# Tree-masked attention: normalising all slots in one operation and overwriting the exchanged halves

## The chip, the cores and the metric

The kernel runs on one core of a Trainium2 chip. The metric is device time in microseconds for one execution. A profile of one execution is at hand for the kernel before; its lines name the engines PE (TensorE matmul), PEld (TensorE weight load), DVE (VectorE), ACT (ScalarE), POOL (GpSimd) and SP (SyncE).

## The reference

The problem is attention with a fixed mask. There are 8 batches of 12 heads, 512 positions and 64 features per head. Positions are the nodes of a binary heap, and a position sees itself and its ancestors only.

```python
for i in range(seq):
    mask[i, i] = 1
    parent = i
    while parent > 0:
        parent = (parent - 1) // 2
        mask[i, parent] = 1
scores = np.einsum('bhqd,bhkd->bhqk', Q, K) * scale
scores = scores + (1 - mask) * (-1e9)
weights = np.exp(scores - np.max(scores, axis=-1, keepdims=True))
weights = weights / (np.sum(weights, axis=-1, keepdims=True) + 1e-10)
return np.einsum('bhqk,bhkd->bhqd', weights, V).astype(np.float32)
```

## The kernel before

Query `n = 4p + t` lies on partition `p` (0 to 127) in slot `t` (0 to 3). Two heads of one batch are worked on together. Such a couple is called a pair: 8 batches of 6 pairs make 48, numbered by `i`, and `hp` is the pair's number within its batch.

For each pair there are three functions:

- `transposes(i)` turns Q and K of the pair with 16 TensorE matmuls against permutation matrices (L274). VectorE copies the Q result to `qt` (L296), ScalarE the K result to `kt` (L297). At the first pair of a batch it also issues the batch's loads (`load`, L223) on POOL's queue: Q and K by parts of the heads, V one batch ahead, with a cast from fp32 to bf16.
- `scores(i)` makes masked scores for a shared set of 128 keys (`st1`) and for four further sets, one for each column block (`stx`). A matmul with code matrices writes a large negative number where the mask forbids (L310). ScalarE takes the exponentials into `et1` (L323) and `etx` (L334).
- `values(i)` multiplies the exponentials with V into one PSUM tile `o2` (32 matmuls, L352). V has a column of ones beside its 64 features, so each slot gets 65 columns, the last of them the sum of the weights. VectorE takes the reciprocals of the 8 sums of each partition (`rec`, L358). It multiplies each slot's 64 features by them into the fp32 tile `of` (L364). SP's queue writes `of` to the output (L369).

The queries' columns have one peculiarity. On partitions 0 to 63, columns 0 and 1 are exchanged:

```python
def _slot(c, p):

    return 1 - c if c < 2 and p < 64 else c
```

The normalisation at L361 to L368 puts them back in order, with one operation for columns 2 and 3 of all partitions, one for columns 0 and 1 of partitions 64 to 127, and one for columns 0 and 1 of partitions 0 to 63 in reversed order.

VectorE also spreads V into the tiles `v1` and `vx` for the next batch (`spread` and `copies`, L259): ten copies over six pairs.

The order on PE, VectorE, ScalarE and POOL is the program's own (`manual_schedule`). For each `i` it is `scores(i + 1)`, `transposes(i + 3)`, `values(i)`, then a share of the spread copies. The PSUM pools have one buffer for each tile, so the matmuls of `values(i + 1)` wait until the multiplies of `values(i)` have read `o2`. The pool of `rec` and `of` has four buffers, the pool of loaded Q, K and V six, and the spread V tiles are three.

Of the kernel before, what the change touches and what calls it, by code (L numbers as in the profile page):

```python
# [126 lines left out]
def kernel(  # L127
# [8 lines left out]
    B, H, S, D = Q.shape  # L136
    P = nc.NUM_PARTITIONS
# [203 lines left out]
    def values(i):  # L341
        b, hp = pairs[i]
        v1, vx = v1s[b % NV], vxs[b % NV]
        et1, etx = state.pop(i)
        o2 = psumO.tile([P, 2, 512], fp32)
        for hi in range(2):
            h = 2 * hp + hi
            for t in range(T):
                w = [(et1[:, hi, P * t:P * t + P], v1[:, h, 0:D + 1]),
                     (etx[:, hi, t, :], vx[:, h, t, 0:D + 1])]  # L350
                for n, (e, v) in enumerate(w):
                    nc.tensor.matmul(  # L352
                        out=o2[:, hi, (D + 1) * t:(D + 1) * (t + 1)],
                        lhsT=e, rhs=v, start=n == 0, stop=n == len(w) - 1,
                    )
        o4 = o2[:, :, 0:T * (D + 1)].rearrange("p h (t x) -> p h t x", t=T)
        rec = opool.tile([P, 2, T, 1], fp32)
        nc.vector.reciprocal(out=rec[:, :, :, :], in_=o4[:, :, :, D:D + 1])  # L358
        of = opool.tile([P, 2, T * D], fp32)
        of4 = of[:, :, :].rearrange("p h (t d) -> p h t d", t=T)  # L360
        for p0, p1, c0, t0 in ((0, P, slice(2, 4), slice(2, 4)),  # L361
                               (64, P, slice(0, 2), slice(0, 2)),
                               (0, 64, slice(1, None, -1), slice(0, 2))):
            nc.vector.tensor_tensor(  # L364
                out=of4[p0:p1, :, t0, :], in0=o4[p0:p1, :, c0, 0:D],
                in1=rec[p0:p1, :, c0, :].to_broadcast([p1 - p0, 2, 2, D]),
                op=ALU.mult,
            )  # L368
        nc.sync.dma_start(  # L369
            out=out[b, 2 * hp:2 * hp + 2].rearrange(  # L370
                "h (p t) d -> p h (t d)", t=T
            ),
            in_=of[:, :, :],
        )
# [3 lines left out]
    with tc.manual_schedule(engines={E.PE, E.DVE, E.Activation, E.Pool}):  # L378
        transposes(0)
        scores(0)  # L380
        transposes(1)
        copies(spread(0, 0, 6))
        transposes(2)
        for i in range(N):
            b, hp = pairs[i]
            if i + 1 < N:
                scores(i + 1)
            if i + 3 < N:
                transposes(i + 3)
            values(i)  # L390
            if b == 0:
                if hp in (0, 3):
                    todo = spread(0, 6, H) if hp == 0 else spread(1, 0, H)
                copies(todo[4 * (hp % 3):4 * (hp % 3) + 4])
            elif b + 1 < B:
                if hp == 0:
                    todo = spread(b + 1, 0, H)
                cuts = (0, 1, 2, 4, 6, 8, 10)
                copies(todo[cuts[hp]:cuts[hp + 1]])
# [30 lines left out]
```

## Time and profile before

| | |
|---|---|
| median of 5 executions | 162.08 us (162.0 to 163.41) |
| the profiled execution | 161.85 us, of which its span is 159.7 us |
| DVE busy | 128.5 us (80% of the span), 339 instructions |
| PE busy | 110.5 us (69%) |
| ACT busy | 107.9 us (68%) |
| POOL busy | 38.7 us (24%) |
| multiplies of L364 | 144, 60.9 us busy |
| bytes moved by the DMA engines | 32.28 MB |

The span runs from the first to the last instruction. The device time of the same execution is 2.15 us longer. A row of digits in the profile cuts the span into 40 equal slices and gives the busy share of each slice in tenths. A row of a group gives, behind its name, tiles and shape, the number of instructions, then the busy time in us and the mean in ns, then the idle time of the engine just before them and what ended it. A row of a timeline gives the start, the duration, the engine, the line and the tiles, and in brackets how long the engine had been idle and what released it. In a merged row (x3) the duration runs from the first start to the last end.

### The profile page before, as it was taken

To read this page: it belongs to the slowest core of one execution; us is meant where nothing else is said; L and a number is where in the kernel's file an instruction comes from. 1 tells how busy PE (TensorE), PEld (TensorE's weight loads), DVE (VectorE), ACT (ScalarE), POOL (GpSimd) and SP (SyncE) were. 2 spreads that over 40 slices of the span, in tenths; PEclk is the share of its full clock that TensorE was granted. 3 is DMA by queue.
4 is the path that set the end of the run, shared out by engine and by line. 5 is a ranking of instruction groups with operands and counts; after the bars stand their busy time and mean duration, and the time that the engine had idled before them with its cause. 6 is when DMAs were issued, how large, how long until landed. Compare 5 with 4: busy or idle time off the path is not lost.

```text
span 159.7 us, 5230 instructions
## 1 busy us (share of the span) xinstructions
PE 110.5 (69%) x2208; PEld 78.3 (49%) x2208; DVE 128.5 (80%) x339; ACT 107.9 (68%) x145; POOL 38.7 (24%) x49
## 2 busy tenths in 40 slices
PE   0427598658787769776885598776977788679630
PEld 0214375445555546554664376554655565546320
DVE  2108579899899989997999869998999899987751
ACT  3142467684598679956987568867996698759810
POOL 7955441422212322033222242223201000000000
PEclk9999999996999999999999969999999999999995
DMA  5999999999999999999999999999999999331331
GB/s 132 125 179 197 197 199 219 224 221 219 222 233 231 235 230 226 238 231 231 223 233 232 226 239 221 223 236 226 224 240 224 235 226 234 119 135 66 135 131 66
DMA packets 50951, 32.28 MB, mean 202 GB/s; under 512 B 1520, under 2 KB 50800, under 8 KB 50928
## 3 DMA queue, kind: packets, MB, share of 16 engines
q0 software_dynamic: 37584, 18.88, 87.7%
q1 hardware_dynamic: 13344, 13.08, 28.5%
q8 instruction: 17, 0.28, 0.6%
q14 instruction: 6, 0.05, 0.1%
HBM read 38.24 MB, written 12.58 MB: 318 GB/s over the span
## 4 chain that ended last, share of the span: by engine, by line
DMA 54%; DVE 30%; PE 7%; issue 5%; POOL 2%; DVEq 0%; POOLq 0%
DMA ks<-in_K_dram 54%; DVE of L364 18%; PE o L352 5%; DVE vx L259 4%; DVE rec L358 3%; DVE v L259 3%; DVE qt L296 2%; POOL qs L223 1%; PE st L310 1%; POOL vs L223 1%; PE tk L274 0%; POOL ks L223 0%; PE stx L310 0%; PE tq L274 0%; DVEq L425 0%
## 5 line engine op out<-in xcount | busy, mean ns | idle before, releaser
L323 ACT ACTIVATE et<-st 128x1024 bf16<-128x1024 f32 x48 | 49.2, 1024 | 29.5 <-PE st L310 28.7
L364 DVE TENSOR_TENSOR of<-o,rec 128x256 f32<-128x256 f32 x144 | 60.9, 423 | 3.0
L352 PE MATMUL o<-v,et 128*128 128x65 bf16 x384 | 30.9, 196 | 25.5 <-DVE of L364 19.6
L352 PEld LDWEIGHTS <-et 128*128 128x128 bf16 x384 | 25.1, 98 | 32.9 <-DVE of L364 23.6
L334 ACT ACTIVATE etx<-stx 128x768 bf16<-128x768 f32 x48 | 38.6, 804 | 0.0
L297 ACT COPY kt<-tk 128x512 bf16<-128x512 bf16 x48 | 28.4, 591 | 14.3 <-PE tk L274 14.3
L352 PE MATMUL o<-vx,etx 128*128 128x65 bf16 x384 | 30.6, 195 | 0.0
L296 DVE COPY qt<-tq 128x512 bf16<-128x512 bf16 x48 | 20.3, 423 | 12.4 <-PE tq L274 11.2
L274 PE MATMUL tq<-ptile,qs 128*64 128x128 bf16 x384 | 21.4, 237 | 12.3 <-DMA qs<-in_Q_dram 8.7
L259 DVE COPY vx<-vs 32x1536 bf16<-32x1536 bf16 (+3 forms) x54 | 28.3, 525 | 1.2
L352 PEld LDWEIGHTS <-etx 128*128 128x128 bf16 x384 | 25.8, 99 | 0.0
L274 PE MATMUL tk<-ptile,ks 128*64 128x128 bf16 x384 | 20.8, 231 | 6.3 <-DMA ks<-in_K_dram 6.0
L310 PEld LDWEIGHTS <-kt 64*128 64x128 bf16 x480 | 19.2, 99 | 10.8 <-issue 2.2
L223 POOL DMA_DIRECT2D qs<-in_Q_dram x18 | 15.1, 840 | 36.2 <-DMA vs<-in_V_dram 15.7
L274 PEld LDWEIGHTS <-qs 128*64 128x64 bf16 x384 | 14.9, 116 | 15.8 <-DMA qs<-in_Q_dram 9.6
L223 POOL DMA_DIRECT2D ks<-in_K_dram x18 | 14.8, 825 | 30.1 <-DMA ks<-in_K_dram 11.1
L310 PE MATMUL st<-ctile 64*128 64x512 bf16 x96 | 19.8, 409 | 0.0
L310 PE MATMUL st<-qt,kt 64*128 64x512 bf16 x96 | 19.5, 402 | 0.1
L274 PEld LDWEIGHTS <-ks 128*64 128x64 bf16 x384 | 14.9, 117 | 7.8 <-DMA ks<-in_K_dram 7.4
L358 DVE RECIPROCAL rec<-o 128x8 f32<-128x8 f32 x48 | 9.6, 200 | 9.8 <-PE o L352 9.8
L310 PE MATMUL stx<-qt,kt 64*128 64x96 bf16 x384 | 17.0, 211 | 0.0
L310 PE MATMUL stx<-ctile 64*128 64x384 bf16 x96 | 16.7, 343 | 0.0
(11 smaller groups left out, 33.5 us busy)
## 6 DMA issues: line engine op xcount, KB each, us to landing
out_dram<-of SPq DMA_DIRECT2D x48, 256.0 KB, 6.2
qs<-in_Q_dram POOLq DMA_DIRECT2D x14, 384.0 KB, 26.3
ks<-in_K_dram POOLq DMA_DIRECT2D x14, 384.0 KB, 26.5
vs<-in_V_dram POOLq DMA_DIRECT2D x7, 768.0 KB, 27.6
vs<-in_V_dram POOLq DMA_DIRECT2D x2, 384.0 KB, 9.0
qs<-in_Q_dram POOLq DMA_DIRECT2D x2, 256.0 KB, 17.1
ks<-in_K_dram POOLq DMA_DIRECT2D x2, 256.0 KB, 17.5
ctile<-tree_codes SPq DMA_DIRECT2D x1, 288.0 KB, 2.8
```

What stands on the lines that cost most here:

```text
L223: nc.gpsimd.dma_start(out=dst[:, h0:h1, :], in_=src[n, h0:h1].rearrange("h (p t) d -> p h (t d)", t=T),)
L259: nc.vector.tensor_copy(out=o, in_=i)
L274: nc.tensor.matmul(out=o[D * hi:D * hi + D], rhs=perms[mat], lhsT=src[:, 2 * hp + hi, D * t:D * t + D], start=True, stop=True, is_transpos ...
L296: nc.vector.tensor_copy(out=qt[:, :], in_=tq[:, :])
L297: nc.scalar.copy(out=kt[:, :].rearrange("d (i j x) -> d i j x", j=2, x=32), in_=tk[:, :].rearrange("d (j i x) -> d i j x", j=2, x=32)[:, 0:8],
L310: nc.tensor.matmul(out=dst, lhsT=lhsT, rhs=rhs, start=first, stop=True, skip_group_check=not first,)
L323: nc.scalar.activation(out=et1[:, :, :], in_=st1[:, :, :], func=AF.Exp, scale=scale)
L334: nc.scalar.activation(out=etx[:, :, :, 32:P], in_=stx[:, :, 0:384].rearrange("p h (c q) -> p h c q", c=T), func=AF.Exp, scale=scale,)
L352: nc.tensor.matmul(out=o2[:, hi, (D + 1) * t:(D + 1) * (t + 1)], lhsT=e, rhs=v, start=n == 0, stop=n == len(w) - 1,)
L358: nc.vector.reciprocal(out=rec[:, :, :, :], in_=o4[:, :, :, D:D + 1])
L364: nc.vector.tensor_tensor(out=of4[p0:p1, :, t0, :], in0=o4[p0:p1, :, c0, 0:D], in1=rec[p0:p1, :, c0, :].to_broadcast([p1 - p0, 2, 2, D]), ...
```

## The change

Two of the three multiplies are merged. One operation now normalises all four slots of all 128 partitions, in the columns' own order. On partitions 0 to 63 this leaves columns 0 and 1 in each other's slots. A second operation then writes these two slots of partitions 0 to 63 again, in reversed order, over what the first wrote.

```diff
-        for p0, p1, c0, t0 in ((0, P, slice(2, 4), slice(2, 4)),
-                               (64, P, slice(0, 2), slice(0, 2)),
+        for p0, p1, c0, t0 in ((0, P, slice(0, 4), slice(0, 4)),
                                (0, 64, slice(1, None, -1), slice(0, 2))):
             nc.vector.tensor_tensor(
                 out=of4[p0:p1, :, t0, :], in0=o4[p0:p1, :, c0, 0:D],
-                in1=rec[p0:p1, :, c0, :].to_broadcast([p1 - p0, 2, 2, D]),
+                in1=rec[p0:p1, :, c0, :].to_broadcast([p1 - p0, 2, t0.stop, D]),
                 op=ALU.mult,
             )
```

## The prediction

> **What bounds the kernel now.** I read the page first: the span, the busy shares and the two rows of slices (each slice is 159.7 / 40 = 4.0 us).
>
> ```profile
> span 159.7 us, 5230 instructions
> ...
> PE 110.5 (69%) x2208; PEld 78.3 (49%) x2208; DVE 128.5 (80%) x339; ACT 107.9 (68%) x145; POOL 38.7 (24%) x49
> ...
> DVE  2108579899899989997999869998999899987751
> ...
> DMA  5999999999999999999999999999999999331331
> ```
>
> Two things are nearly full at once: the transfers until slice 34 (136 us), and VectorE over most of the same stretch. Only where VectorE is what ends last does a shorter normalisation count. So I asked for the groups with shapes kept apart, to price an operation, and for VectorE's timeline, to see how operations follow one another.
>
> ```profile
> L364 DVE TENSOR_TENSOR of<-o,rec 64x256 f32<-64x256 f32 x96 | 40.5, 422 | 1.3
> ...
> L364 DVE TENSOR_TENSOR of<-o,rec 128x256 f32<-128x256 f32 x48 | 20.4, 424 | 1.6
> ```
>
> Half the partitions cost the same: 422 against 424 ns. What counts is elements per partition, 256 in each of the three.
>
> ```profile
> 68.69 0.42 DVE L296 COPY qt<-tq 128x512 bf16<-128x512 bf16 x1
> 69.03 0.20 DVE L358 RECIPROCAL rec<-o 128x8 f32<-128x8 f32 x1
> 69.26 1.30 DVE L364 TENSOR_TENSOR of<-o,rec 128x256 f32<-128x256 f32 x3
> 70.48 0.70 DVE L259 COPY v<-vs 32x768 bf16<-32x768 bf16 x2
> ...
> 145.56 0.21 DVE L358 RECIPROCAL rec<-o 128x8 f32<-128x8 f32 x1 [0.42 <-PE o L352]
> 145.81 1.30 DVE L364 TENSOR_TENSOR of<-o,rec 128x256 f32<-128x256 f32 x3
> ```
>
> Three multiplies take 1.30 us, so 3 x 0.424 and about 13 ns between them. The reciprocal starts 0.34 us after a copy of 0.42 us: it depends on nothing in it and overlaps it by 0.08 us. The multiply that reads `rec` starts 0.03 us after the reciprocal has ended.
>
> Then TensorE, for what holds it, late in the run:
>
> ```profile
> 125.41 0.41 PE L274 MATMUL tk<-ptile,ks 128*64 128x128 bf16 x8 [0.75 <-DMA ks<-in_K_dram]
> 126.06 0.20 PE L352 MATMUL o<-v,et 128*128 128x65 bf16 x1 [0.24 <-DVE v L259]
> ...
> 144.87 0.20 PE L352 MATMUL o<-v,et 128*128 128x65 bf16 x1 [0.19 <-DVE of L364]
> ...
> 149.45 0.20 PE L352 MATMUL o<-v,et 128*128 128x65 bf16 x1 [0.76 <-DVE of L364]
> ```
>
> At 125.4 us it waits for a K load (batch 6, heads 6 to 11: issued at 97.22, 28.1 us to landing, so 125.3). The same wait stands at 74.07 (1.58 us) and 91.23 (1.72 us). From there to the end its waits are for VectorE. The chain of waits gives one period of the end, 145.54 to 147.83: PE `o` 0.67, `rec` 0.22, the multiplies 1.30, joints 0.10, together 2.29 us with nothing beside it, since `o` has one buffer.
>
> So: up to pair 36 (batch 6, `hp` 0) the loads set the pace at the middle of each batch, VectorE in between. POOL issues a new load about 0.5 us after an older one lands, with some 25 us of loads queued, so a faster VectorE cannot pull loads forward. From pair 36 on VectorE sets the end.
>
> **The change part by part.** Per pair, removed: three multiplies of 256 elements per partition. Added: A, all partitions, 512 elements; C, partitions 0 to 63, 256 elements, on top of what A wrote. Elements per partition stay at 768; one instruction's fixed part goes. C is the old third multiply, 0.424.
>
> A has no row. By the trace, its floor is the line through the reciprocal (8 elements, 198 ns) and the multiply: 0.91 ns an element, so 657 ns; its ceiling is twice 424, 848 ns. [...]
>
> The joint between A and C is the unknown. C overwrites A, so an order between them may be enforced by a wait on VectorE's own count. Nearest row: reciprocal to multiply, +0.03 us after the end. If no wait is made, both start at partition 0 and the nearest row is copy to reciprocal, -0.08. I take +0.03: 0.691 + 0.030 + 0.424 = 1.145 us against 1.299, **0.154 us saved per pair**. With -0.08 it would be 1.035, 0.264 saved. Queued behind C on VectorE are the spread copies, the next `qt` and the next reciprocal; waiting for C are `values` of the next pair on PE and the output DMA on SP. All move earlier by the saving.
>
> [...]
>
> In all VectorE is relieved of 48 x 0.154 = 7.4 us. What reaches the end:
> - Pairs 0 to 35: nothing. The loads cover it: the K loads for pairs 18, 24 and 36 already arrive after TensorE asked for them, and the one for pair 30 lands at 108.1 where its scores' turn comes at about 109. If that cover were gone, 36 x 0.154 = 5.5 us more.
> - Pair 36: its K transposes end at 125.41 + 0.41 = 125.82, then 0.24 us of waiting for VectorE's copies, which are now earlier: up to 0.24 gained. Against that, outputs are written earlier and share the DMA engines: at most some 0.6 of a pair's output ahead, and one output takes 0.7 us of all engines (slices of 3 tenths over a 2.3 us period), so 0 to 0.4 us of delay. Net 0.
> - Pairs 36 to 47: 12 x 0.154 = 1.85 us. The next load (K of batch 7, issued 106.18, landing 132.5) allows pair 39's reciprocal from about 133.6; it would come at 134.67 - 3 x 0.154 = 134.2. The last two K loads land at 136.8 and 138.8, needed at 141 and later.
> - Limits in pairs 42 to 44: TensorE has 0.19 us to spare per pair, enough for 0.154 but not 0.264. ScalarE's three operations run back to back there (`et` starts at 143.88, 146.16, 148.46: 2.29 us), so it falls behind by 0.15 a pair; the score buffers are free 0.56 us ahead (`et` read by 144.90, written again at 145.46), enough for three such pairs. After pair 44 there is no `kt` and it has slack again.
>
> Sum: 0 + 1.85, about 1.9 us. The profiled execution took 161.85 us (span 159.7 and 2.15 around it), so 159.95; the median shown is 162.08, 0.23 above it: **160.2 us**.
>
> SP's output issues keep their number and size, POOL has no instruction moved, and `rec` and the DMA wait on the `of` buffer stay ahead of the first multiply.
>
> **The rivals.**
> (a) No wait is made between A and C. 12 x 0.264 = 3.2, less 0.1 each in pairs 42 to 44: 2.9 us, 159.2. For it: that overlap is in the trace between independent operations. Against: A and C write the same bytes, and the one dependent pair that the trace has waits.
> (b) The end is held elsewhere: ScalarE's 2.29 us holds pairs 42 to 44 (0.46 lost) or loads land 0.4 to 0.5 us later. 1.4 us, 160.7. [...]
> [...]
> That the change removes an instruction is plain from the code; it cannot fail to.
>
> **How the numbers follow.** A measurement here tells 0.5%, 0.8 us, from no change. Forecast 0.52; (a) 0.22; (b) at 160.7 0.12; (b) with all its losses 0.09; (c) 0.05. Faster by over 0.5% (below 161.27): 0.52 + 0.22 + 0.12 = 0.86; same 0.09; slower 0.05. The range runs from a little below (a), 158.7, to where (b) has most of its losses, 161.4; only (c) and the ends are left out.
>
> **What would show it.** [...] VectorE busy down by about 48 x 0.157 = 7.5 us to 121. K loads of batches 4 to 6 landing within 0.5 us of 91.2, 108.1 and 125.3, with longer TensorE waits in front of them. Period in the last pairs 2.14 instead of 2.29. I would be wrong if loads landed earlier (a gain near 5 us) or if the joint were above 0.1 us.

## The result

The changed kernel takes 160.9 us (median of 44 executions) against 162.31 us (median of 79). The ratio is 0.9933, 95% interval 0.9916 to 0.995, so about 1.1 us faster. Some executions of every kernel lie over 1.5% above its fastest; the ratios, and the table of profiles below, leave them out. Two later measurements gave 0.9905 (0.9867 to 0.9943) and 0.9893 (0.9848 to 0.9937), 1.5 and 1.7 us. The forecast was 160.2 us, 1.9 us faster. The direction and the range held; the forecast gain was 0.2 to 0.8 us larger than those measured.

From the page of the kernel after: the lines that answer to those shown of before, the group of the K transposes, and the row of TensorE's granted clock (in tenths of full speed, one digit for each 4 us):

```profile
span 159.3 us, 5182 instructions
...
PE 114.3 (72%) x2208; PEld 82.4 (52%) x2208; DVE 121.9 (76%) x291; ACT 107.4 (67%) x145; POOL 37.9 (24%) x49
...
DVE  2109289899699989996799799985899489988651
...
PEclk9999999999599999998799999996999779999975
DMA  5999999999999999999999999999999999332331
...
L274 PE MATMUL tk<-ptile,ks 128*64 128x128 bf16 x384 | 21.4, 236 | 10.4 <-DMA ks<-in_K_dram 10.1
```

The same clock row and the same group in the page of the kernel before:

```profile
PEclk9999999996999999999999969999999999999995
...
L274 PE MATMUL tk<-ptile,ks 128*64 128x128 bf16 x384 | 20.8, 231 | 6.3 <-DMA ks<-in_K_dram 6.0
```

VectorE is relieved: its busy time falls from 128.5 to 121.9 us. The loads end in the same slice, and TensorE waits for K for 10.1 us in all instead of 6.0. What was not expected is in the clock row: more slices in which TensorE ran below full speed. PE is busy for longer (114.3 against 110.5 us) with the same 2208 matmuls.

The two groups of multiplies of the kernel after, by shape:

```profile
L363 DVE TENSOR_TENSOR of<-o,rec 128x512 f32<-128x512 f32 x48 | 33.2, 692 | 1.7
...
L363 DVE TENSOR_TENSOR of<-o,rec 64x256 f32<-64x256 f32 x48 | 20.0, 416 | 1.6
```

The large multiply takes 692 ns where 691 was expected. VectorE's timeline of the kernel after, in the last pairs:

```profile
145.55 0.21 DVE L358 RECIPROCAL rec<-o 128x8 f32<-128x8 f32 x1 [0.42 <-PE o L352]
145.79 1.14 DVE L363 TENSOR_TENSOR of<-o,rec 128x512 f32<-128x512 f32 x2
...
147.69 0.21 DVE L358 RECIPROCAL rec<-o 128x8 f32<-128x8 f32 x1 [0.42 <-PE o L352]
```

The two multiplies take 1.14 us together, in place of 1.30, and one pair follows the other after 2.14 us, in place of 2.29. So the operation and the chain at the end are priced rightly. Yet the profiled span is only 0.4 us shorter.

One term has to be put straight first. A step `i` is the turn of the program's loop that ends in `values(i)`; the transposes in it are those of pair `i + 3`. So what the prediction calls the K load for pair 36 is the load that TensorE waits for in step 36, ahead of `values(36)`; pair 39 is the first to use it. The sums do not depend on the name.

Here is what happened on TensorE, from its timeline after, and below it the last pair's line from the timeline before:

```profile
125.60 0.54 PE L274 MATMUL tk<-ptile,ks 128*64 128x128 bf16 x8 [2.14 <-DMA ks<-in_K_dram]
...
153.49 0.21 PE L352 MATMUL o<-v,et 128*128 128x65 bf16 x1 [1.57 <-DVE of L363]
```

```profile
154.12 0.19 PE L352 MATMUL o<-v,et 128*128 128x65 bf16 x1 [1.72 <-DVE of L364]
```

The K load of step 36 lands about when it did before (125.5 us; 125.3 before), but TensorE now waits 2.14 us for it instead of 0.75. (The loads of steps 24 and 30 land at 90.4 and 107.6 us, against 91.2 and 108.1.) The view by windows shows what follows the waits. A line gives the window, its length, the busy time and instructions of PE, PEld, VectorE, ScalarE and POOL, then the granted clock, the DMA share and GB/s:

```profile
90.40:94.40 4.00, 3.91 (x86) 2.88 (x86) 2.98 (x8) 2.89 (x5) 1.55 (x2) 1.00 1.32 237
107.60:111.60 4.00, 3.99 (x65) 2.90 (x66) 2.30 (x5) 2.60 (x4) 1.07 (x2) 0.64 1.33 238
125.60:129.60 4.00, 4.00 (x59) 2.79 (x60) 2.13 (x5) 1.98 (x3) 0.00 (x0) 0.57 1.30 243
129.60:133.60 4.00, 3.96 (x92) 2.96 (x89) 3.45 (x9) 3.65 (x6) 0.00 (x0) 1.00 1.30 231
153.40:154.60 1.20, 1.04 (x16) 0.90 (x16) 0.03 (x1) 0.00 (x0) 0.00 (x0) 0.50 0.27 96
```

Behind waits of 2.47 us (at 107.6) and 2.14 us (at 125.6) the clock is 0.64 and 0.57 over 4 us; behind one of 1.46 us (at 90.4) it is 1.00. In the last pair it is 0.50: its value matmuls take 1.05 us instead of 0.66. There the wait is not longer than before (1.57 against 1.72 us), so length alone cannot be the cause. The kernel before had one such stretch late in the run, at 91.2.

### The profile page after: what moved, and what is told of

It is laid out like the page before. It is cut to its first block, busy times and chain, and to the rows that moved or that the text cites. A ratio compares the mean times of both kernels' runs of the same rounds, so it can differ in the third digit from the quotient of the medians.

```text
span 159.3 us, 5182 instructions
## 1 busy us (share of the span) xinstructions
PE 114.3 (72%) x2208; PEld 82.4 (52%) x2208; DVE 121.9 (76%) x291; ACT 107.4 (67%) x145; POOL 37.9 (24%) x49
## 4 chain that ended last, share of the span: by engine, by line
DMA 74%; DVE 10%; PE 7%; POOL 3%; issue 3%; POOLq 0%
DMA qs<-in_Q_dram 40%; DMA ks<-in_K_dram 34%; DVE of L363 6%; PE o L352 4%; PE st L310 1%; DVE vx L259 1%; DVE rec L358 1%; POOL vs L223 1%; POOL qs L223 1%; POOL ks L223 1%; DVE v L259 1%; PE stx L310 1%; PE tk L274 1%; PE tq L274 1%; DVE qt L296 1%
## 5 line engine op out<-in xcount | busy, mean ns | idle before, releaser
L363 DVE TENSOR_TENSOR of<-o,rec 128x512 f32<-128x512 f32 x96 | 53.2, 554 | 3.3
L352 PE MATMUL o<-v,et 128*128 128x65 bf16 x384 | 32.7, 201 | 18.1 <-DVE of L363 11.8
L352 PEld LDWEIGHTS <-et 128*128 128x128 bf16 x384 | 26.7, 102 | 25.4 <-DVE of L363 16.2
L352 PE MATMUL o<-vx,etx 128*128 128x65 bf16 x384 | 32.4, 200 | 0.0
L274 PE MATMUL tq<-ptile,qs 128*64 128x128 bf16 x384 | 21.9, 240 | 11.6 <-DMA qs<-in_Q_dram 7.4
L274 PE MATMUL tk<-ptile,ks 128*64 128x128 bf16 x384 | 21.4, 236 | 10.4 <-DMA ks<-in_K_dram 10.1
L352 PEld LDWEIGHTS <-etx 128*128 128x128 bf16 x384 | 27.6, 102 | 0.0
L223 POOL DMA_DIRECT2D qs<-in_Q_dram x18 | 14.6, 813 | 35.5 <-DMA qs<-in_Q_dram 9.6
L274 PEld LDWEIGHTS <-ks 128*64 128x64 bf16 x384 | 15.4, 120 | 11.9 <-DMA ks<-in_K_dram 11.5
```

Source lines behind the costliest of these rows:

```text
L223: nc.gpsimd.dma_start(out=dst[:, h0:h1, :], in_=src[n, h0:h1].rearrange("h (p t) d -> p h (t d)", t=T),)
L274: nc.tensor.matmul(out=o[D * hi:D * hi + D], rhs=perms[mat], lhsT=src[:, 2 * hp + hi, D * t:D * t + D], start=True, stop=True, is_transpos ...
L352: nc.tensor.matmul(out=o2[:, hi, (D + 1) * t:(D + 1) * (t + 1)], lhsT=e, rhs=v, start=n == 0, stop=n == len(w) - 1,)
L363: nc.vector.tensor_tensor(out=of4[p0:p1, :, t0, :], in0=o4[p0:p1, :, c0, 0:D], in1=rec[p0:p1, :, c0, :].to_broadcast([p1 - p0, 2, t0.stop, ...
```

## The experiments

Three theories of the missing part were tried. Theory 1: the clock falls behind the longer waits for K. Theory 2: the loads land later, since outputs are written earlier. Theory 3: it is mainly the last pair's slow matmuls. ("Rival 3" in e2 and e3 is another idea: that the pairs before 36 carry the gain.)

**e1, the change again.**

> The changed kernel again, beside which the others of this group are read. Theory 1 (clock): the longer waits for K loads let TensorE's granted clock fall to about half for some 4 us afterwards, and this takes back part of the 1.85 us; the time is 0.6 to 0.8% below before. In the profile the waits of TensorE for K at pairs 18, 24, 30 and 36 are 1.5 to 2.5 us, and the windows of 4 us behind those over about 1.9 us have a clock near 0.6. Theory 2 (loads): the clock plays no part; the K loads of batches 5 to 7 land 0.5 us or more later than in the kernel before and every window has a clock of 1.

Measured: ratio 0.9905. Its profile has clocks of 0.53 and 0.50 behind waits for K of 2.42 and 2.32 us, and 1.00 behind one of 0.92. K lands at 90.7, 108.3 and 124.8 us (91.2, 108.1 and 125.3 before): no delay by 0.5 us. One execution of each would be thin evidence, since the load of step 36 lands anywhere between 124.6 and 127.4 us in the fourteen profiles. But its mean is 125.7 us in the four kernels whose first 36 pairs are the old ones and 125.8 in the other ten, so nothing supports theory 2. Over the executions of this group the mean clock was 0.947 with the change and 0.966 before.

**e2, the change in pairs 36 to 47 only, and e3, in pairs 0 to 35 only** (`i < 36` in the same line; `old` holds the three multiplies, `new` the two).

```diff
-        for p0, p1, c0, t0 in ((0, P, slice(0, 4), slice(0, 4)),
-                               (0, 64, slice(1, None, -1), slice(0, 2))):
+        for p0, p1, c0, t0 in (new if i >= 36 else old):
```

> The change for pairs 36 to 47 only; pairs 0 to 35 have the three old multiplies. Theory 1 (clock): up to pair 36 the waits for K stay as short as before, so the clock falls no more often than before, and the 12 pairs bring 1.85 us less at most 0.4 for a slow last pair: 1.4 to 1.9 us faster than before, 0.3 to 0.8 us faster than the full change. Theory 2 (loads): outputs of the first 36 pairs are no longer early, so loads land as before: the full 1.85 us as well, but the clock is the same in both kernels. Rival 3 (the early pairs carry the gain): under 0.4 us faster than before.

> The change for pairs 0 to 35 only; pairs 36 to 47 have the three old multiplies. Theory 1 (clock): no gain from the pairs themselves, and slower stretches behind longer waits for K: 0.3 us faster to 1 us slower than before, with a clock near 0.6 in two or more of the windows behind the K waits of pairs 18, 24, 30 and 36. Theory 2 (loads): 0 to 0.5 us slower with the clock at 1. Rival 3 (the early pairs carry the gain): 1 us or more faster than before.

Measured: e2 0.9949 (0.9916 to 0.9982), e3 1.0032 (0.9996 to 1.0067). The 36 early pairs alone bring nothing, as the forecast had it for them; whether they lose is within the interval. The mean clock of e3 is 0.951, and its profile has clocks of 0.72 and 0.57 behind waits for K of 2.66 and 1.95 us. Rival 3 falls. But e2 is 0.8 us faster, not 1.4 to 1.9, and not faster than the full change. In its profile the stretch is as expected, with the clock whole in both places that the full change had lost:

```profile
125.90:128.40 2.50, 2.46 (x55) 1.78 (x56) 1.40 (x5) 1.45 (x2) 0.00 (x0) 1.00 1.32 235
152.62:154.00 1.38, 0.64 (x16) 0.52 (x16) 0.67 (x2) 0.00 (x0) 0.00 (x0) 1.00 0.45 161
```

That execution had a mean clock of 0.98; the mean over e2's executions is 0.966, and those with a higher clock were the faster ones (correlation with the span -0.70). The profile shows a better case than the median. The mean clock does not settle it, though: 0.966 is that of the kernel before as well, and over the 39 executions of the change that the first ratio counts the correlation is only -0.29.

**e4, fillers for TensorE in all these places; e5, at the K waits only; e6 and e10, ahead of the last pair only.** (In the first part of the diff `i` is the pair that is transposed: steps 18, 24, 30 and 36.)

```diff
+        if i in (21, 27, 33, 39):
+            for n in range(20):
+                put(tk[:, 0:128], qs, n % T, 0)
         for t in range(T):
             at = kput[t][1]
...
+        if i == N - 1:
+            tq = psumT.tile([P, 512], bf16)
+            for n in range(16):
+                for hi in range(2):
+                    nc.tensor.matmul(
+                        out=tq[D * hi:D * hi + D, 0:128], rhs=perms[0],
+                        lhsT=loaded[b][0][:, 2 * hp + hi, 0:D],
+                        start=True, stop=True, is_transpose=True,
+                    )
         o2 = psumO.tile([P, 2, 512], fp32)
```

> The full change, plus filler matmuls on TensorE: 40 repeated transposes of Q into the K tile ahead of the K transposes issued at pairs 18, 24, 30 and 36 (overwritten by them), and 32 into a tile that nothing reads ahead of the last pair's value matmuls. They take about 1.4 and 1.1 us and fill part of the waits. Theory 1 (clock): no wait of TensorE over 1.3 us there, the clock stays at 1, and the time falls by 0.8 to 1.4 us against the full change, 2 to 2.5 us below before. Theory 2 (loads): the time is that of the full change within 0.3 us, since the loads land when they land.

> The full change with the fillers ahead of the K transposes only (pairs 18, 24, 30, 36); nothing ahead of the last pair. Theory 1 (clock): most of the loss of the full change arises at the K waits, so this is 0.3 to 0.8 us faster than the full change, with the last pair's value matmuls still slow (about 1.0 us for 16 pairs of matmuls) in executions where the clock has fallen. Rival (only the last pair matters): the time of the full change.

> The full change with the filler ahead of the last pair's value matmuls only. Theory 1 (clock): 0.2 to 0.4 us faster than the full change (the last pair's matmuls in 0.66 us instead of 1.05), the waits for K and the slow stretches behind them as in the full change. Rival (only the last pair matters): as fast as with all fillers, about 1.3% below before.

Measured: e4 0.9874 (0.9834 to 0.9914), 159.47 us, with all its executions within 159.1 to 160.0; e5 0.9911 (0.9878 to 0.9944); e6 0.9873 (0.9825 to 0.9921). With both fillers the gain is 2.0 us, that of the forecast, but only some 0.5 us more than e1's beside it, where 0.8 to 1.4 was expected. The clock behaves: of the eight K waits in the profiles of e4 and e5, seven are followed by a clock of 1.00 and one by 0.88 (in e4, where the clock had already fallen behind a wait for VectorE just before), while six of eleven in three profiles of the change (the first one, e1 and e9 below) are followed by 0.5 to 0.75. e4's mean clock is 0.975. But e5 alone is no faster than the change, against theory 1, and e6 alone looks as fast as e4, in favour of theory 3. The intervals of all of them overlap with e1's. The kernel of e6 was measured again as e10; e4 was measured once only.

**e7, the kernel before with the same fillers (in steps 18 and 24, and ahead of the last pair).**

> The kernel before with fillers: 40 repeated transposes ahead of the K transposes issued at pairs 18 and 24 (overwritten by them) and 32 into a tile that nothing reads ahead of the last pair. Theory 1 (clock): its waits for K are shorter (1.6 and 1.7 us) and its clock falls less often, so there is less to win than in the full change: 0.2 to 0.6 us faster than before. Theory 2 (fillers help for a reason apart from the change): as much as in the full change, 0.7 us or more.

Measured: 1.0015 (0.9977 to 1.0052). The fillers win nothing that can be told in the kernel before: at most 0.4 us by the interval, and not 0.7.

**e8, the second multiply into a tile of its own** (the exchanged halves stay exchanged, so the output is not the reference's).

```diff
+        ox = opool.tile([P, 2, 2 * D], fp32)
+        ox4 = ox[:, :, :].rearrange("p h (t d) -> p h t d", t=2)
...
+            to = of4 if p1 == P else ox4
             nc.vector.tensor_tensor(
-                out=of4[p0:p1, :, t0, :], in0=o4[p0:p1, :, c0, 0:D],
+                out=to[p0:p1, :, t0, :], in0=o4[p0:p1, :, c0, 0:D],
```

> The full change, but the second multiply writes a tile of its own that nothing reads: the exchanged halves stay exchanged in the output. Joint theory (the 0.03 us between the two multiplies is a wait made because they write the same bytes): here the second starts 0.05 to 0.09 us before the end of the first, the two take 1.03 to 1.06 us instead of 1.14, and the time is 0 to 1 us below the full change (12 pairs by 0.1, less what TensorE's clock takes). Rival (the joint is a fixed gap of the engine): 1.14 us as before and the same time.

VectorE's timeline of e8:

```profile
144.87 0.69 DVE L366 TENSOR_TENSOR of<-o,rec 128x512 f32<-128x512 f32 x1
145.48 0.41 DVE L366 TENSOR_TENSOR ox<-o,rec 64x256 f32<-64x256 f32 x1
```

The second starts 0.08 us before the first has ended, and the two take 1.02 us. In the kernel after it starts 0.03 us behind the end in all 48 pairs. So the 0.03 us joint of the change is a wait that comes of writing over the first multiply's output, as the forecast took it, and rival (a)'s price was right for a case that the change isn't. The time did not follow: 0.9891 (0.9842 to 0.994), no different from the change. Yet the profile's stretch from pair 36's reciprocal to the end is 29.50 us, 1.56 shorter than the 31.06 of e2 and e4 in the table further down. The mean clock in e8 is the lowest of all kernels, 0.928; whether that is where the gain went is not shown.

**e9, the change; e10, with the filler ahead of the last pair; e11, the change from pair 36 on with that filler.** The edits are those of e6 and e2.

> The changed kernel again, beside which this group is read: 0.6 to 1% faster than before. Two places where TensorE's clock can take back a part of the 1.85 us are still open: behind the K waits (theory 1) and in the last pair (theory 3).

> The full change with the filler ahead of the last pair's value matmuls, a second time, for more executions. Theory 3 (most of what is missing is the last pair's slow matmuls): 0.4 to 0.8 us faster than the full change, about 1.2% faster than before. Theory 1 (most is missing behind the K waits): 0 to 0.3 us faster than the full change.

> The change for pairs 36 to 47 only, with the filler ahead of the last pair. Theory 3 (last pair): 1.8 to 2.1 us faster than before, the whole of the 12 pairs' 1.85 and the same as the full change with this filler; with pair 36 on, the stretch from the landing of its K load to the end of the span is about 32 us, against 34.4 before. Theory 1 (K waits): faster than the full change with this filler by 0.3 us or more, since the early pairs do not lengthen the waits.

Measured: e9 0.9893 (0.9848 to 0.9937), e10 0.9917 (0.9877 to 0.9957), e11 0.9893 (0.9836 to 0.995). The lead of e6 did not come back; theory 3 as the main cause isn't supported by time. No two of these three kernels can be told apart. In e11 the stretch from the landing of the K load of step 36 to the end was expected at about 32 us; it is 33.9 (125.6 to 159.5).

The profile of e9 shows that the length of a wait does not decide alone. Its waits for K in steps 30 and 36, of 2.36 and 2.32 us, left the clock whole, and the one of 1.57 us ahead of the last pair found it at half. The traces show what goes with it. Within an execution the granted clock, once it has changed, changes again only after 3.41 us or a multiple of it: in the kernel after at 40.42, 43.83, 74.55, 77.96, 108.68, 112.09, 125.75, 129.16 and 153.05 us, between 1.00 and 0.50. Here are two such periods of the kernel after, then two of e9, around the K wait of step 30:

```profile
105.27:108.68 3.41, 1.07 (x26) 0.90 (x28) 1.70 (x5) 1.60 (x3) 1.51 (x2) 1.00 1.33 233
108.68:112.09 3.41, 3.41 (x48) 2.40 (x46) 2.27 (x5) 2.20 (x3) 0.74 (x1) 0.50 1.36 225
```

```profile
104.61:108.02 3.41, 1.87 (x38) 1.20 (x38) 3.25 (x8) 2.26 (x4) 0.92 (x2) 1.00 1.35 221
108.02:111.43 3.41, 2.41 (x54) 1.75 (x54) 1.77 (x5) 1.35 (x2) 0.75 (x1) 1.00 1.33 234
```

In the kernel after, the wait of 2.47 us falls into one period: PE is busy for 1.07 of 3.41 us, and the next period has half the clock. In e9 the wait of 2.36 us lies across two periods, each has PE busy for more than half, and the clock stays. The fourteen traces have 494 periods at full clock, up to the last matmul. PE was busy for less than 0.45 of the period in 32 of them, and half the clock followed each time; it was busy for more than 0.505 in 448, and half the clock never followed. Between these it went both ways (11 of 14). Where the periods lie differs from execution to execution, so a wait of the same length costs clock in one and not in another. It is so in the last pair too. The kernel after has PE busy for 1.68 us from 149.64 to 153.06, a share of 0.49, and its value matmuls begin at 153.49, at half. The kernel before has 2.19 us from 149.40 to 152.82, a share of 0.64, and the matmuls behind its longer wait, from 154.12 us on, run at a clock of 1.00.

**e12, a version meant to beat both**: the change with 24 filler matmuls ahead of the last pair, and no second multiply in the last three pairs; four transfers put the halves in place instead.

```diff
+        for p0, p1, c0, t0 in whole if last else whole + swap:
...
+        q = nc.scalar if i == N - 1 else nc.sync
+        nc.sync.dma_start(out=dst[64:P], in_=of[64:P, :, :])
+        q.dma_start(out=dst[0:64, :, 0:D], in_=of[0:64, :, D:2 * D])
+        nc.sync.dma_start(
+            out=dst[0:64, :, 2 * D:4 * D], in_=of[0:64, :, 2 * D:4 * D])
+        q.dma_start(out=dst[0:64, :, D:2 * D], in_=of[0:64, :, 0:D])
```

> A version meant to beat both: the full change with the filler (24 matmuls) ahead of the last pair, and in the last three pairs no second multiply: the first multiply's tile is written out by four transfers that put the exchanged halves in place, since the transfers have room by then. Three pairs lose 0.45 us each from the chain, so 1.2 us less than the full change with the filler, if the four transfers end no later than one; 0 or slower if their issues or their pieces of 256 bytes hold the end by 1 us.

Measured: 0.9934 (0.9892 to 0.9975), no better than the change. SP's timeline shows why:

```profile
153.74 0.61 SPq L386 DMA_DIRECT2D out_dram<-of  x1
154.39 0.60 SPq L388 DMA_DIRECT2D out_dram<-of  x1
155.09 0.59 SPq L384 DMA_DIRECT2D out_dram<-of  x1
155.73 0.61 SPq L386 DMA_DIRECT2D out_dram<-of  x1
```

The last multiply ended at 152.41 + 0.69 = 153.10 us, but SP was still issuing the transfers of the pair before, one every 0.65 to 0.70 us, and reached the last pair's only at 155.09. The chain was shortened and the issue queue became the end.

## Why the prediction was right, and where its size was off

One sum settles it. From the start of pair 36's reciprocal (VectorE's timeline) to the end of the span, in the profiles:

| kernel | multiplies from pair 36 on | clock behind the K wait of step 36, and in the last pair | us |
|---|---|---|---|
| before | three | 1.00, 1.00 | 32.95 |
| e3 | three | 1.00, 1.00 | 33.08 |
| e2 | two | 1.00, 1.00 | 31.06 |
| e4 | two | 1.00, 1.00 | 31.06 |
| e9 | two | 1.00, 0.50 | 31.54 |
| after | two | 0.53, 0.50 | 32.13 |

(The clock is over 2.5 us behind the wait, and over the last pair's value matmuls. e7, three multiplies and the clock whole, has 32.91; e5 and e11, two and whole, have 31.13, as has e1, with 0.70 in the last pair.)

- **The price of the change, 0.154 us a pair on 12 pairs, 1.85 us:** measured 32.95 - 31.06 = 1.89 where the clock is whole. Right, with each of its parts: 692 ns, a joint of 0.03 us, a period of 2.14 us. The forecast's 0.691 us for the large multiply is shown by no run of before, whose trace gives only the estimated bounds of 657 and 848 ns; the profile after has 692 ns in its place.
- **Pairs 0 to 35 at nothing:** right, by e3. The saving turns into longer waits of TensorE for K (10.1 us in all, 6.0 before).
- **Pair 36, "net 0":** in the profile after, this is the term that failed. It counted what VectorE's copies and the outputs' traffic would do to the start of pair 36, and left every matmul at its old duration. In the profile after, pair 37's reciprocal comes 2.99 us after pair 36's; with the clock whole (e2) 2.34. That is 0.65 us, and none in the executions where the clock holds. Ahead of it, from the start of the K transposes to pair 36's reciprocal, the times are 1.34 us before, 1.04 in e2, e4 and e9, and 1.57 after. So with the clock whole the gain of up to 0.24 us was there (0.30); with the clock at half the same stretch is 0.53 us longer, and the gain is gone. The delay of 0 to 0.4 us set against it does not show in the mean landing of the load (125.7 and 125.8 us, under e1).
- **The last pair:** the same omission. From pair 46's reciprocal to 47's it is 2.61 us after and 2.21 in e2: 0.40 us. With the 0.65 this makes 1.05, and 32.13 - 31.06 = 1.07. From the K transposes to the end the clock took 1.6 us: it is 34.29 us before, 32.10 in e2 and e4, 33.70 after. The K transposes start 0.19 us later after (125.60 against 125.41), and 0.59 less 0.19 is the 0.4 us by which the span is shorter.
- **The rest of the way to the median:** the change's gain over three measurements is 1.1 to 1.7 us, 0.2 to 0.8 short. In size the clock can be the whole of it. From the K transposes of step 36 on, the three profiles of the change (after, e1, e9) lose 1.6, 0.07 and 0.48 us against e2 and e4, 0.7 on average. But these are three executions, and the times do not prove it: e2 has the mean clock of the kernel before and is only 0.8 us faster. The mean clock is also a poor measure, since it counts falls that the loads cover: e1's clock fell at 73.9 and 108.0 us, and e1 still has 31.13. Some of the spread is in the loads, whose landing moves by 2.8 us with nothing changed in how they are issued. So the cause of the missing part is shown for the profile after, and open for the median. How it is shared between the K waits and the last pair is open too: e5, e6 and e10 do not tell it apart.
- **Limits in pairs 42 to 44:** TensorE's spare time was put at 0.19 us, and ScalarE was said to fall behind by 0.15 us a pair, since its three operations seemed to fill the period of 2.29. That reading was wrong, at no cost to the sum. ScalarE keeps up, as its timeline after shows:

```profile
144.02 1.02 ACT L323 ACTIVATE et<-st 128x1024 bf16<-128x1024 f32 x1 [0.92 <-PE st L310]
...
146.15 1.02 ACT L323 ACTIVATE et<-st 128x1024 bf16<-128x1024 f32 x1
...
148.29 1.02 ACT L323 ACTIVATE et<-st 128x1024 bf16<-128x1024 f32 x1
```

These are 2.13 and 2.14 us apart. TensorE's spare time is used up: the chain of waits after runs from one `o` to the next in 2.13 us without a wait.

```profile
142.72 0.66 PE o L352 x16
...
144.59 0.24 PE tk L274 x8
144.83 0.02 issue
144.85 0.66 PE o L352 x16
```

This is not TensorE's limit, though. In e8, where VectorE's chain is shorter, the same way takes TensorE 2.05 us (`o` at 144.00 and at 146.05). So VectorE's 2.14 us sets the pace there.

Of the rivals, (a) fell by the joint, and e8 shows what it would have been. (b) named ScalarE or later loads as what holds the end elsewhere. The size came out near it (160.7 forecast, 160.9 measured), but by luck: ScalarE kept up, and the loads did not land later. No run shows the losses behind the range's end at 161.4 us either; the period in the last pairs fell by 0.15 us, from 2.29 to 2.14. (c), the slower kernel that was given 0.05, fell, and no run shows a price for it: the second multiply starts 0.03 us behind the first in all 48 pairs, and the kernel is 1.1 to 1.7 us faster.

## What to carry to other kernels

When one engine's work is shortened where another resource sets the pace, ask what the freed time becomes: here it became longer idle stretches of TensorE (10.1 us of waiting for K, 6.0 before), and some of those cost clock afterwards. Ask for each whether it can bring TensorE's busy share of one period of 3.41 us below half (here half the clock followed all 32 periods with less than 0.45, and none of the 448 with more than 0.505), and whether what follows is on the path to the end. Price the merge of operations by its fixed part (here 0.156 us for the one saved: twice 424 less 692 ns) and count only the instances behind the last point where loads pin the schedule. Measure such a gain from a pinned event to the end of the span as well as by whole times, since the pin itself (the landing of the K load) moves by 2.8 us from run to run.

## What the runs showed of the hardware that was not expected

- TensorE's clock fell to half for 3.41 us (twice that in three cases ahead of the last pair) behind periods of 3.41 us in which PE was busy for less than about half: behind all 32 with a share below 0.45, 11 of 14 between that and 0.505, and none of 448 above (fourteen traces, under e9). So it was at half after waits of 1.41 us (at 39.76 us, after) to 2.47 us (at 107.61, after), and whole after 2.32 to 2.46 us in other places (e9).
- With transposes alone as fillers in the waits for K the clock was 1.00 behind seven of eight of them and 0.88 behind the other (e4, e5). In e4 TensorE ran nothing but transposes from 88.64 to 92.17 us, at 0.50 from 88.79 on and at 1.00 from 92.20 on.
- The second multiply, which overwrites a part of what the first wrote, starts 0.03 us after its end (48 of 48, after); writing another tile it starts 0.08 us before the end (e8).
- In e12 SP needed 0.64 to 0.77 us from one issue of an output transfer to the next, with 32, 64 and 128 KB alike. The eight of pairs 45 and 46 take 5.4 us, from 149.68 to 155.09, while pair 47's multiply ends 3.45 us after pair 45's.
